# A 1024 x 1024 output projection done with seven block products in place of eight, and a norm's vector kept on chip

## The chip, the cores and the metric

The kernel runs on one core of one Trainium2 chip. A core has TensorE (PE, matrix products into PSUM; PEld is its weight load), VectorE (DVE), ScalarE (ACT), GpSimd (POOL) and SyncE (SP, which here only issues transfers). The metric is the device time of one execution in microseconds (us); lower is better.

## The reference, cut to what matters

One encoder layer is applied to two request groups with the same weights: Prompt (1024 tokens) and Sample (512 tokens), 1024 channels wide, all in float32. The part that the change touches is the end of the layer.

```python
def rms_norm(x, g):
    return x * lax.rsqrt(jnp.mean(x * x, axis=-1, keepdims=True) + EPS) * g
...
    merged = jnp.zeros_like(x)
    for n in range(N_BRANCH):                       # pooling, self-attention, cross-attention
        merged = merged + gates[:, :, n] * (branches[n] @ w_branch[n])    # (L, 512) @ (512, 1024)

    y = rms_norm(merged @ w_out, ln_post)           # (L, 1024) @ (1024, 1024)
    return x + y
```

## The kernel before

Each float32 operand of a product is split into a high part in TensorE's faster format (written by ScalarE, `L168`) and the rest, the low part (written by VectorE as operand minus high part, `L165`). A product then is three matmuls: high x high, high x low, low x high (`mm3`, each 128 x 128 against 128 x 512). `weights` loads a tile of 128 x 1024 weights from memory (`raw<-wt`, `L142`) and splits it into `whi` and `wlo`.

The program is written as one stream of Python generators; a scheduler turns it into a fixed order of instructions for each engine, and every engine works through its own order without overtaking. Priorities (`tc.high_priority`: AHEAD for weight splits, EVAC for emptying PSUM, LATER behind other work) and the number of buffers of each tag (`u`: NU = 7, `med`: NM = 14, `hu`: NHU = 9, `raw`: NRAW = 3, `whi`/`wlo`: NW = 2, `kt`: 4) decide that order. PSUM has three two-bank tiles A and two one-bank tiles B.

The order of the stages is: memory tokens, Prompt's input projections (`products`, which already uses the seven-product form, with additions on the weights in `additions`), Sample's input projections and Prompt's attention woven together, then three blocks of 512 tokens: two of Prompt, one of Sample. A block is `branches` / `merge` (24 steps of 12 matmuls: a step's product, then on VectorE gate times product, `L1080`, then on GpSimd the sum over the branches into `acc`, `L1082`), and `out_phase` (the output projection).

For a Prompt block, `out_phase` takes the output channels in two halves of 512. For each half it goes through four weight tiles (`half`), two k-chunks of 128 channels in each, and four tiles of 128 tokens: 2 x 8 x 4 x 3 = 192 matmuls. `evacuate` multiplies a finished PSUM tile by `lnpost` on VectorE (`L1112`) and squares and sums it on ScalarE (`L1113`). `finish` makes the norm's factor (`L1099`, then GpSimd `L196`, `L200`), multiplies and adds the residual (`L1106`) and stores. The merged operand reaches `out_phase` as eight chunks, split two at a time as they get ready (`split_pair`). `lnpost` is loaded and scaled in each of the three blocks (`L1095`). Sample's block ends in `ending`.

## Time and profile before

| | |
|---|---|
| median of 3 runs | 1457.52 us (1455.51 to 1458.99) |
| the profiled execution | 1455.05 us, of which 1452.8 us are the span that the profile covers |
| mean granted TensorE clock | 0.998 |
| busy share PE / DVE / ACT / POOL | 98% / 67% / 49% / 19% |
| the output projections of Prompt's two blocks | 1183.4 to 1227.0 us and 1292.2 to 1335.8 us of the span |

In the profile an instruction is named by its line, its engine, and output<-input with buffer numbers left out. `med` is a general 128 x 2048 tile: activations, gates, sums and their parts. In the output projection before, `A<-whi,med` is a matmul with a weight part and an activation part. Durations overlap: an instruction's successor on the same engine can start before its recorded end, so the cost of one in a row of many is the distance between starts.

### The profile page before, as it was taken

The numbers are of one execution on the slowest core, as the hardware profiler recorded it, in microseconds if no ns is written. First come the engines' busy times: TensorE is split into PE (matmuls) and PEld (weight loads), VectorE is DVE, ScalarE is ACT, GpSimd is POOL, SyncE is SP. The second block draws the span as 40 slices with busy tenths as digits, with TensorE's granted clock in tenths as the row PEclk, the third lists the DMA queues.
The fourth block names the chain that finished last, engine by engine and source line by source line (L and its number), as shares of the span: only waits on it lengthen the run. The fifth ranks groups of instructions, "written<-read, shape, count | busy, mean of one in ns | idle before, by whom it ended". The sixth has DMA issues, their size and how long they took to land. (4 is left out here: it accounts for less than half of the span.)

```text
span 1452.8 us, 19525 instructions
## 1 busy us (share of the span) xinstructions
PE 1429.2 (98%) x7264; PEld 1198.1 (82%) x7264; DVE 968.9 (67%) x1211; ACT 711.6 (49%) x1085; POOL 276.9 (19%) x286
## 2 busy tenths in 40 slices
PE   7989999999999999999999999999999999999998
PEld 6868888888888888788888888888888888888887
DVE  7996685766547664665777667686676665765764
ACT  6454444444434444443666666676676223323222
POOL 1000110200000000210223332343333230240231
PEclk9999999999999999999999999999999999999999
DMA  8313243332322444244645665565357735945942
GB/s 301 115 60 104 77 138 115 111 123 68 130 97 67 153 140 136 82 157 163 244 187 196 217 231 191 196 224 176 133 170 262 270 121 184 335 161 186 330 139 82
DMA packets 95375, 238.65 MB, mean 164 GB/s; under 512 B 10672, under 2 KB 18992, under 8 KB 95280
## 3 DMA queue, kind: packets, MB, share of 16 engines
q1 hardware_dynamic: 86064, 203.84, 41.5%
q10 hardware_dynamic: 9216, 33.56, 6.0%
q8 instruction: 57, 0.93, 0.3%
q14 instruction: 38, 0.31, 0.1%
HBM read 151.38 MB, written 52.43 MB: 140 GB/s over the span
## 5 line engine op out<-in xcount | busy, mean ns | idle before, releaser
L129 PE MATMUL B<-med,whi 128*128 128x512 f32 x1576 | 493.7, 393 | 5.5 <-DVE med L165 3.0
L129 PE MATMUL A<-med,whi 128*128 128x512 f32 x1200 | 374.1, 392 | 1.6 <-ACT med L168 1.0
L129 PEld LDWEIGHTS B<-med,whi 128*128 128x128 f32 x1576 | 291.9, 188 | 66.0 <-DVE med L165 4.1
L168 ACT ACTIVATE whi<-raw 128x1024 fp32r<-128x1024 f32 (+1 forms) x169 | 167.4, 991 | 289.7 <-PE A L129 137.3
L129 PE MATMUL B<-med,wlo 128*128 128x512 f32 x788 | 308.5, 391 | 0.0
L165 DVE TENSOR_TENSOR wlo<-raw,whi 128x1024 fp32r<-128x1024 f32 (+1 forms) x169 | 211.9, 1255 | 134.7 <-ACT whi L168 133.2
L129 PEld LDWEIGHTS A<-med,whi 128*128 128x128 f32 x1200 | 223.4, 188 | 48.7 <-ACT med L168 1.2
L129 PE MATMUL A<-med,wlo 128*128 128x512 f32 x600 | 234.1, 390 | 0.0
L129 PEld LDWEIGHTS B<-med,wlo 128*128 128x128 f32 x788 | 148.2, 188 | 31.2
L196 POOL TENSOR_SCALAR s<-s 128x16 f32<-128x16 f32 (+3 forms) x17 | 7.5, 442 | 659.1 <-DVE s L591 324.9
L129 PEld LDWEIGHTS A<-med,wlo 128*128 128x128 f32 x600 | 112.8, 188 | 23.9 <-DVE wlo L165 0.2
L165 DVE TENSOR_TENSOR med<-A,med 128x1024 fp32r<-128x1024 f32 (+1 forms) x93 | 112.9, 1215 | 27.7 <-ACT med L168 26.1
L168 ACT ACTIVATE med<-A 128x1024 fp32r<-128x1024 f32 x92 | 94.2, 1025 | 69.2 <-PE A L133 68.8
L823 POOL TENSOR_SCALAR u<-u,s 128x1024 f32<-128x1024 f32 x64 | 72.1, 1126 | 211.9 <-DVE s L822 174.6
L819 DVE TENSOR_REDUCE s<-A 128x1 f32<-128x1024 f32 x64 | 77.8, 1216 | 37.0 <-PE A L129 35.4
L1082 POOL TENSOR_TENSOR med<-med,med 128x512 f32<-128x512 f32 x48 | 75.8, 1592 | 128.0 <-DVE med L1080 90.7
L129 PE MATMUL A<-whi,med 128*128 128x512 f32 (+1 forms) x352 | 98.3, 360 | 0.0
L821 ACT ACTIVATE u<-A,s 128x1024 f32<-128x1024 f32 x64 | 71.4, 1115 | 40.6 <-issue 23.4
L129 PE MATMUL A<-kt,med 128*128 128x512 f32 x320 | 87.8, 395 | 0.0
L168 ACT ACTIVATE whi<-sum 128x1024 fp32r<-128x1024 f32 x50 | 53.1, 1062 | 67.2 <-PE B L129 40.2
L165 DVE TENSOR_TENSOR med<-med,med 128x1024 fp32r<-128x1024 f32 (+1 forms) x50 | 55.1, 1115 | 33.0 <-ACT med L168 29.2
L129 PE MATMUL B<-med,vt 128*128 128x256 f32 x512 | 74.6, 286 | 1.3 <-DVE med L165 1.2
(197 smaller groups left out, 1884.6 us busy)
## 6 DMA issues: line engine op xcount, KB each, us to landing
raw<-wt SPq DMA_DIRECT2D x168, 512.0 KB, 3.7
u<-u ACTq DMA_DIRECT2D x64, 512.0 KB, 3.1
merge<-hu SPq DMA_DIRECT2D x72, 256.0 KB, 2.1
med<-merge SPq DMA_DIRECT2D x72, 256.0 KB, 5.6
med<-br SPq DMA_DIRECT2D x36, 256.0 KB, 5.4
q<-hu SPq DMA_DIRECT2D x24, 256.0 KB, 2.5
br<-hu SPq DMA_DIRECT2D x24, 256.0 KB, 2.9
med<-q SPq DMA_DIRECT2D x12, 512.0 KB, 4.6
```

The source lines that it names most:

```text
L129: pe.matmul(out, l, r, **k)
L165: v.tensor_tensor(out, x, hi.bitcast(F32), op=ALU.subtract)
L168: act.activation(hi, x, AF.Copy)
L196: pool.tensor_scalar(ss, ss, EPS, 1.0, op0=ALU.add, op1=ALU.mult)
L819: v.reduce_max(mx[:], a[:], axis=AX.X, negate=True)
L821: act.activation(p, a[:], AF.Exp, bias=mx[:], accum_out=sm[:])
L823: pool.tensor_scalar(p, p, rc[:], 1.0, op0=ALU.mult, op1=ALU.mult)
L1082: pool.tensor_tensor(at, at, sg, op=ALU.add)
```

## The change

It has two parts. First, for Prompt's two blocks `out_phase` is replaced by `out_products`. Merged (512 tokens x 1024 channels) is taken as four quarters of 256 tokens x 512 channels (a11, a12, a21, a22), the weights as four quarters of 512 x 512, and the result is put together from seven products of quarters. A product is 2 weight tiles x 2 tiles of 128 tokens x 2 k-chunks x 3 = 24 matmuls, 168 in a block. The products need four sums of quarters on the activations (`total`, VectorE, `L1153`), which are then split (`quarter_parts`), and four sums on the weights. The weight sums are computed once, by `out_weights`, as a background task in Prompt's input projections (8 loads, 8 VectorE additions of 128 x 1024, 8 stores to scratch `wsum`), and loaded back in each block by `right`. Partial results are kept in `hu` tiles by ScalarE (`keep`, `L1179`) or added on VectorE (`put`, `L1188`), squared on ScalarE (`L1189`), and multiplied by `lnpost` on GpSimd (`L1190`). The split of the merged operand leaves `merge` except for a11 (`by_quarters`). Second, `lnpost` is loaded and scaled once, into a `sum` tile (`gain`).

```diff
         def gate_to_scratch(m, c0):
             def take(i, j, b, s):
+                if T == 1024 and (m, c0, i, j) == (0, 2, 0, 0):
+                    tasks.append(out_weights())
...
+    wsum = {i: scratch(f"wsum_{i}", [P, 2 * D]) for i in (2, 3, 4, 6)}
+    def out_weights():
+        for c in range(2):
+            b11, b12, b21, b22 = [U() for _ in range(4)]
+            for x, half, k in ((b11, 0, 0), (b12, 1, 0), (b21, 0, 2), (b22, 1, 2)):
+                load(x, wt[TILES["half", half, k + c]])
+            for _ in range(4):
+                yield
+            v.tensor_tensor(b12, b22, b12, op=ALU.subtract)
+            v.tensor_tensor(b11, b12, b11, op=ALU.add)
+            yield
+            v.tensor_tensor(b22, b22, b11, op=ALU.subtract)
+            v.tensor_tensor(b21, b21, b11, op=ALU.subtract)
+            yield
+            for i, x in ((4, b12), (2, b11), (3, b22), (6, b21)):
+                nc.sync.dma_start(wsum[i][:, c * D:(c + 1) * D], x)
...
-        yield from out_phase(merged, xs[g][bs, :], ys[g][bs, :], last)
+        yield from (out_phase if last else out_products)(merged, xs[g][bs, :], ys[g][bs, :])
...
+    def by_quarters(d, acc, merged):
+        if d == 3:
+            merged.append(quarter_parts(quarter(acc, 0, 0)))
+        elif d == 7:
+            merged.append([quarter(acc, i, j) for i in range(2) for j in range(2)])
...
+    def out_products(merged, src, dst):
+        yv, ssq, lnpost = out_tiles()
+        first, (a11, a12, a21, a22) = merged
...
+        def left(i):
+            if i == 1:
+                return quarter_parts(a12)
+            if i == 2:
+                total(3, a21, a22, ALU.add)
+                total(2, sums[3], a11, ALU.subtract)
+            elif i == 4:
+                total(4, a11, a21, ALU.subtract)
+            elif i == 5:
+                total(5, a12, sums[2], ALU.subtract)
+            return quarter_parts(a22 if i == 6 else sums[i])
+        def right(i, c):
+            raw, t = sb.tile([P, D], F32, tag="kt", bufs=4, name=nm("w")), M()
+            load(raw[:], wsum[i][:, c * D:(c + 1) * D] if i in wsum else wt[TILES["half", int(i == 5), c + 2 * (i > 0)]])
+            with tc.high_priority(AHEAD):
+                split(t[:, :D], t[:, D:], raw[:])
...
+        def put(t, n, b, k):
...
+                if k is None:
+                    act.activation(x, b, AF.Copy)
+                else:
+                    v.tensor_tensor(x, b, kept.pop(k)[:], op=ALU.add)
+                act.activation(junk[:], x, AF.Square, scale=0.25 * D ** -0.5, accum_out=ssq[:, t, n:n + 1])
+            pool.tensor_tensor(x, x, lnpost[:, ns], op=ALU.mult)
+        for i in range(7):
+            lhs, bank = ahead, "XYXZXZX"[i]
...
+            for c in range(2):
+                w = right(i, c)
+                if c == 0 and i < 6:
+                    ahead = left(i + 1)
+                for u in range(2):
...
+        for i in range(2):
+            finish(i, yv, ssq, src, dst)
```

How the order of instructions moves is shown at three places of Prompt's first block; the second has the same order.

VectorE, from the gating of the last two merge steps into the output projection. Before (`med_10766` is the low part of merged's last two chunks, `wlo` are weights' low parts):

```order
L1080 SCALAR_TENSOR_TENSOR med_10647<-med_10647,B_10736 128x512
L1080 SCALAR_TENSOR_TENSOR med_10647<-med_10647,A_10751 128x512
L165 TENSOR_TENSOR wlo_10810<-raw_10807,whi_10809 128x1024
L165 TENSOR_TENSOR med_10766<-med_10203,med_10766 128x2x512
L165 TENSOR_TENSOR wlo_10840<-raw_10837,whi_10839 128x1024
L165 TENSOR_TENSOR wlo_10870<-raw_10867,whi_10869 128x1024
L165 TENSOR_TENSOR wlo_10915<-raw_10912,whi_10914 128x1024
L1112 TENSOR_TENSOR med_10769<-A_10775,u_10772 128x512 x2
```

After (`med_10238` and `med_10239` are `acc`; `L1153` are the sums of quarters; `w` is a loaded weight tile; `med_10809` is a12's low part, `med_10825` that of product 0's second weight tile, `med_10848` and `med_10872` those of product 1's two weight tiles):

```order
L1102 SCALAR_TENSOR_TENSOR med_10680<-med_10680,A_10781 128x512
L165 TENSOR_TENSOR wlo_11199<-raw_11196,whi_11198 128x1024
L1153 TENSOR_TENSOR u_10852<-med_10238,med_10239 128x1024
L165 TENSOR_TENSOR med_10809<-med_10239,med_10809 128x1024
L165 TENSOR_TENSOR med_10825<-w_10824,med_10825 128x1024
L165 TENSOR_TENSOR med_10848<-w_10847,med_10848 128x1024
L1153 TENSOR_TENSOR u_10854<-u_10852,med_10238 128x1024
L1153 TENSOR_TENSOR u_10944<-med_10238 128x1024
L1153 TENSOR_TENSOR u_10987<-med_10239,u_10854 128x1024
L165 TENSOR_TENSOR med_10856<-u_10854,med_10856 128x1024
L165 TENSOR_TENSOR med_10872<-w_10871,med_10872 128x1024
```

Nine rows now stand between the gating of the last merge step (with one prefetched split, `wlo_11199`, behind it) and the low part of product 1's second weight tile; the first of them, and all sums, need the complete `acc`.

TensorE at the same place. Before, the last merge matmuls and the first of the projection:

```order
L129 MATMUL A_10751<-med_10603,wlo_10733 128x512
L129 MATMUL A_10751<-med_10603,whi_10732 128x512 x2
L129 MATMUL A_10751<-med_10603,wlo_10733 128x512
L129 MATMUL A_10775<-whi_10779,med_10644 128x512
L129 MATMUL A_10775<-wlo_10780,med_10644 128x512
L129 MATMUL A_10775<-whi_10779,med_10644 128x512 x2
L129 MATMUL A_10775<-wlo_10780,med_10644 128x512
```

After, products 0 and 1 (the name behind the arrow is the weight tile, with both its parts; the second is the activation tile):

```order
L129 MATMUL A_10781<-med_10639,wlo_10763 128x512
L129 MATMUL A_10802<-med_10805,med_10719 128x512 x6
L129 MATMUL A_10803<-med_10805,med_10719 128x512 x6
L129 MATMUL A_10802<-med_10825,med_10719 128x512
L129 MATMUL A_10803<-med_10825,med_10719 128x512
L129 MATMUL B_10845<-med_10848,med_10809 128x512
L129 MATMUL B_10846<-med_10848,med_10809 128x512
L129 MATMUL A_10802<-med_10825,med_10719 128x512 x5
L129 MATMUL A_10803<-med_10825,med_10719 128x512 x5
L129 MATMUL B_10845<-med_10848,med_10809 128x512 x5
L129 MATMUL B_10846<-med_10848,med_10809 128x512 x5
L129 MATMUL B_10845<-med_10872,med_10809 128x512
```

The matmuls of product 0's second weight tile (`med_10825`) and of product 1 follow product 0's first twelve directly; the first of the five (`x5`) is the one that needs a low part.

VectorE at the end of the output projection. Before (`med_11076` and `med_11079` are the low parts of the next block's branch operand):

```order
L1112 TENSOR_TENSOR med_10770<-A_10776,u_10772 128x512
L165 TENSOR_TENSOR med_11076<-med_11068,med_11076 128x2x512
L165 TENSOR_TENSOR med_11079<-med_11068,med_11079 128x2x512
L165 TENSOR_TENSOR wlo_10975<-raw_10972,whi_10974 128x1024
L165 TENSOR_TENSOR wlo_11005<-raw_11002,whi_11004 128x1024
L165 TENSOR_TENSOR wlo_11088<-raw_11085,whi_11087 128x1024
L1112 TENSOR_TENSOR med_10769<-B_10909,u_10772 128x512
L1112 TENSOR_TENSOR med_10769<-B_10910,u_10772 128x512
L1099 TENSOR_REDUCE s_11044<-s_10771 128x2
L1106 SCALAR_TENSOR_TENSOR u_11048<-med_10769,s_11044,u_11048 128x1024
```

After (`med_11148` and `med_11151` are the same low parts, `L1188` adds the two tiles of product 5):

```order
L165 TENSOR_TENSOR med_11050<-w_11049,med_11050 128x1024
L165 TENSOR_TENSOR med_11075<-w_11074,med_11075 128x1024
L165 TENSOR_TENSOR med_11092<-w_11091,med_11092 128x1024
L1188 TENSOR_TENSOR med_10796<-B_10937,hu_10927 128x512
L1188 TENSOR_TENSOR med_10796<-A_10938,hu_10935 128x512
L165 TENSOR_TENSOR med_11148<-med_11140,med_11148 128x2x512
L1226 TENSOR_REDUCE s_11116<-s_10798 128x2
L1233 SCALAR_TENSOR_TENSOR u_11120<-med_10796,s_11116,u_11120 128x1024
L165 TENSOR_TENSOR med_11151<-med_11140,med_11151 128x2x512
```

The low parts of the next block's operand stood ahead of the second half's evacuations; now they stand behind the last addition, and the second one also behind the first multiplication of `finish` (`L1233`), which waits for GpSimd.

More of the change, by code (lines that the diff above doesn't have):

```diff
@@ L1045, in rest @@
                     chunk(order[order.index(n) + 1], d - 2)
-                yield from merge(n, d, gates.pop(i), br, acc, merged if n == order[-1] else None)
+                yield from merge(n, d, gates.pop(i), br, acc, merged, parts if n == order[-1] else None)
         return [partial(chunk, order[0], c) for c in range(4)] + [partial(gate, i) for i in range(2)], rest()
@@ L1092, in out_phase @@
         ssq = S(16)[:].rearrange("p (t q) -> p t q", t=TT)
[L1093 to L1107 removed]
+        if not gain:
+            gain.append(SUM())
+            load(gain[0][:], rows[0:1, 0:D].partition_broadcast(P))
+            v.tensor_scalar_mul(gain[0][:], gain[0][:], 0.25)
@@ new lines, in finish, with out_phase @@
+    def finish(i, yv, ssq, src, dst):
+        ss = S(2)
+        v.reduce_sum(ss[:], ssq[:, 2 * i:2 * i + 2, :2], axis=AX.X)
+        rstd_of(ss[:])
+        with tc.high_priority(-LATER):
+            for j in range(2):
+                t = 2 * i + j
+                x = U()
+                load(x, src[t * P:(t + 1) * P, :])
+                v.scalar_tensor_tensor(x, yv[i][:, j], ss[:, j:j + 1], x, op0=ALU.mult, op1=ALU.add)
+                nc.sync.dma_start(dst[t * P:(t + 1) * P, :], x)
+    def out_phase(merged, src, dst):
+        yv, ssq, lnpost = out_tiles()
@@ L1146, in out_phase @@
-        for i in range(2):
-            finish(i)
+        o = [a[:, i * BLK:(i + 1) * BLK] for a in (A(), A()) for i in range(2)]
+        for c in range(4):
+            w = weights("half", 0, c)
+            for pair in ((0, 1), (2, 3)):
+                for kk in range(2):
+                    k, s = c * 2 + kk, slice(kk * BLK, kk * BLK + BLK)
+                    for t in pair:
+                        ts = slice(t * P, (t + 1) * P)
+                        mm3(o[t][:], (merged[k][0][:, ts], merged[k][1][:, ts]), w(s), k == 0, k == KC - 1)
+                if c == 3:
+                    for t in pair:
+                        evacuate(t, slice(0, BLK), o[t][:], 0)
+                yield
@@ new lines, in out_phase @@
+        av = A()[:].rearrange("p (t n) -> p t n", t=TT)
+        for c in range(2):
+            w = weights("out", 0, c)
+            for kk in range(4):
+                k, s = c * 4 + kk, slice(kk * 256, kk * 256 + 256)
+                for t in range(TT):
+                    ts = slice(t * P, (t + 1) * P)
+                    mm3(av[:, t], (merged[k][0][:, ts], merged[k][1][:, ts]), w(s),
+                        k == 0 and t % 2 == 0, k == KC - 1 and t % 2 == 1)
+                yield
+        for t in range(TT):
+            evacuate(t, slice(512, 768), av[:, t], 1)
@@ L1149, in ending @@
+        yield from ending(merged, src, dst, yv, ssq, lnpost)
     def ending(merged, src, dst, yv, ssq, lnpost):
```

105 lines of the change are left out of this document (54 added, 51 removed).

## The prediction

> **What bounds the kernel now.** I read the page's busy times first, then a table of stretches around Prompt's output projections, then who waited for whom on PE.
>
> ```profile
> span 1452.8 us, 19525 instructions
> PE 1429.2 (98%) x7264; PEld 1198.1 (82%) x7264; DVE 968.9 (67%) x1211; ACT 711.6 (49%) x1085; POOL 276.9 (19%) x286
> ```
>
> ```profile
> core 0: us, PE busy (x) PEld busy (x) DVE busy (x) ACT busy (x) POOL busy (x), PEclk, DMA share, GB/s
> 285.00:345.00 60.00, 60.00 (x278) 49.66 (x277) 35.77 (x50) 26.49 (x39) 4.88 (x5) 1.00 0.31 101
> 1183.40:1227.00 43.60, 43.60 (x194) 36.13 (x193) 20.36 (x21) 15.28 (x24) 4.24 (x4) 1.00 0.46 152
> 1227.00:1292.40 65.40, 65.40 (x290) 54.17 (x289) 47.44 (x48) 20.15 (x22) 23.62 (x17) 1.00 0.76 274
> 1292.40:1336.00 43.60, 43.55 (x192) 35.72 (x191) 20.36 (x21) 16.02 (x24) 4.20 (x5) 1.00 0.46 156
> ```
>
> ```profile
> PE B L129 <- ACT med L168: 0.9, 1, 0.9
> PE B L129 <- DVE med L165: 0.8, 1, 0.8
> ```
>
> In both projections (second and fourth stretch) PE is busy throughout at full clock, DVE for 20.4 of 43.6 us, ACT for 15.3. The last two rows are all that PE waited from 1090 us to the end. So matmuls set the time there, and each one removed is worth a full slot, as long as PE still waits for nothing. A slot comes from the first matmuls of the two projections, one block (192 + 288 = 480 matmuls) apart:
>
> ```profile
> 1183.39 0.39 PE L129 MATMUL A<-whi,med 128*128 128x512 f32 x1
> 1292.19 0.39 PE L129 MATMUL A<-whi,med 128*128 128x512 f32 x1
> ```
>
> 108.80 / 480 = 0.227 us. The recorded 0.39 would overstate it: it ends 0.16 us after the next one starts.
>
> **Matmuls removed.** 24 in each of two blocks: 24 x 0.227 = 5.4 us a block, 10.9 us in all. The projection would need 168 slots, 38.1 us.
>
> **What DVE and ACT must now do in these 38.1 us.** Prices of rows that stand close in a queue are distances between starts:
>
> ```profile
> 1190.36 1.23 DVE L165 TENSOR_TENSOR med<-med,med 128x1024 fp32r<-128x1024 f32 x1 [2.27 <-ACT med L168]
> 1191.50 1.22 DVE L165 TENSOR_TENSOR wlo<-raw,whi 128x1024 fp32r<-128x1024 f32 x1
> 1184.89 0.68 DVE L1080 SCALAR_TENSOR_TENSOR med<-med,B 128x512 f32<-128x512 f32 x1
> 1185.49 0.68 DVE L1080 SCALAR_TENSOR_TENSOR med<-med,A 128x512 f32<-128x512 f32 x1
> 1189.27 1.06 ACT L168 ACTIVATE med<-med 128x1024 fp32r<-128x1024 f32 x1 [4.60 <-POOL med L1082]
> 1190.23 1.05 ACT L168 ACTIVATE whi<-raw 128x1024 fp32r<-128x1024 f32 x1
> 1224.62 0.60 ACT L1113 ACTIVATE hu<-B 128x512 f32<-128x512 f32 x1 [1.89 <-DVE med L1112]
> 1225.22 0.60 ACT L1113 ACTIVATE hu<-B 128x512 f32<-128x512 f32 x1
> ```
>
> A long DVE row (128x1024, a low part or a sum of quarters) costs 1.14 us, a short one from PSUM 0.60, a high part on ACT 0.96, a square with its sum 0.60. From the end of a merge to the end of its projection DVE has 13 weights' low parts, 6 activations' low parts and 4 sums, 23 x 1.14 = 26.2, and 6 additions of 0.60: 29.8 us, against 38.1 for PE. By shares it fits. But these rows stand on PE's path in a fixed order, and the eight multiplications by `lnpost` move to GpSimd, whose rows of this kind collide with DVE's:
>
> ```profile
> 1168.10 1.29 POOL L1082 TENSOR_TENSOR med<-med,med 128x512 f32<-128x512 f32 x1 [1.10 <-DVE med L1080]
> 1168.14 2.33 DVE L165 TENSOR_TENSOR wlo<-raw,whi 128x1024 fp32r<-128x1024 f32 x1 [0.18 <-ACT whi L168]
> 1179.11 3.51 POOL L1082 TENSOR_TENSOR med<-med,med 128x512 f32<-128x512 f32 x2 [3.10 <-DVE med L1080]
> 1179.48 2.00 DVE L165 TENSOR_TENSOR wlo<-raw,whi 128x1024 fp32r<-128x1024 f32 x1
> 1185.71 3.52 POOL L1082 TENSOR_TENSOR med<-med,med 128x512 f32<-128x512 f32 x2 [3.09 <-DVE med L1080]
> ```
>
> A low part that starts 0.04 us behind a GpSimd sum takes 2.33 instead of 1.23; a pair of sums with a low part between takes 3.51 instead of 2.6. They take turns: each costs the other up to 1.29 us. The Trainium skill, "SBUF — State Buffer", section "Who interferes with whom", says that a DVE instruction with two SBUF inputs and a GpSimd one that reads SBUF lock each other out for the whole instruction; by that rule every collision would cost the upper end below. These rows agree; how often they meet, no run here shows yet.
>
> So I follow the printed order, counting from T, the end of the last merge matmul's slot (1183.39 before).
>
> *Stall 1, products 0 and 1.* The last merge result leaves PE 0.16 after T, is gated (0.68, to T+0.9) and added on GpSimd (1.29, to T+2.25). The prefetched low part ahead of the sums collides with that and ends at T+3.4. The nine rows that end with the low part of product 1's second weight take 9 x 1.14 = 10.3, to T+13.6 (ACT's high parts run ahead of them). PE has 36 + 2 slots of work before it needs this part: T+8.6. Stall 5.0 us; 4.0 if the collision is not there. Before, `acc` came later still (the pair of sums of 1185.71 ends at T+5.8), but only the last two of eight chunks waited for it.
>
> *Stall 2, products 2 and 3.* DVE's next row, the addition for product 1, waits for PE: 5 slots and 0.16, T+14.9. Then 0.60 + 1.14 + 0.60 + 1.14 + 1.14 = 4.6 to the low part of product 2's second weight, T+19.5. PE has 10 + 12 + 3 slots from T+13.6: T+19.3. The high part for product 3, which PE wants at T+19.0, comes on ACT at T+19.6 (two squares and three high parts after the first addition), so 0.6 us at least; two GpSimd multiplications fall in here, up to 2.6 more on DVE. Bounds 0.6 to 2.8; taken 1.5, one of the two collisions (19.5 + 1.3 - 19.3), since DVE is busy with such rows about two thirds of that time.
>
> *Stall 3, products 5 and 6.* The same pattern around product 4's additions: DVE needs 4.6 from the first one, PE has 21 slots less the 0.16, 4.6. Bounds 0.3 (ACT's chain: 0.60 + 0.60 + 2 x 0.96 + 0.60 + 0.96 = 4.7 against 4.4) to 2.6 with both collisions; taken 1.3, one of them.
>
> *Stall 4, the next block.* Its second branch low part stands behind the first `finish`, which needs GpSimd's multiplications and these:
>
> ```profile
> L200 POOL TENSOR_TENSOR s<-s,mhalf 128x2 f32<-128x2 f32 x3 | 2.1, 705 | 0.2
> L196 POOL TENSOR_SCALAR s<-s 128x2 f32<-128x2 f32 x3 | 0.6, 191 | 78.8 <-DVE s L1099 78.8
> L1106 DVE SCALAR_TENSOR_TENSOR u<-med,s,u 128x1024 f32<-128x1024 f32 x4 | 5.1, 1282 | 2.2 <-POOL s L200 2.2
> ```
>
> From the end of product 6's last low part: addition 0.60, square 0.60, high part 0.96, square 0.60, multiplication 1.29, factor 0.90, `finish` 1.20, low part 1.14: 7.3 us. PE gets there 5.4 (the lead DVE has without collisions) plus 7 slots, 7.0, later. Bounds 0.5 (the 0.3 and the gaps between rows on three engines) to 2.1 (collisions on this chain, less what they take from the lead); taken 1.3, the middle.
>
> **What is costed at nothing.** `out_weights`: 8 x 1.14 = 9.1 us on DVE, 16 transfers of 512 KB on SP, in the first stretch of the table, where DVE is idle for 24.2 of 60 us and DMA is busy for 0.31. SP issues the weights of the following pair only behind the stored gates:
>
> ```profile
> 306.31 0.33 SPq L142 DMA_DIRECT2D raw<-wt  x1
> 313.80 0.41 SPq L142 DMA_DIRECT2D raw<-wt  x1
> 316.02 0.32 SPq L515 DMA_DIRECT2D merge<-hu  x1
> 331.71 1.23 DVE L165 TENSOR_TENSOR wlo<-raw,whi 128x1024 fp32r<-128x1024 f32 x1 [0.17 <-ACT whi L168]
> ```
>
> The loads of 306.31 and 313.80 move behind the store of 316.02; they land some 5 us later and are first needed at 331.71. Nothing, at most 2 us if an evacuation of PSUM is held up behind an addition that waits for its load. If DVE's gaps were not there, the 9.1 us would show. The single `lnpost`: two loads and two DVE scalings less, beside work that PE does not wait for; 0, at most 1 us gained. The weight transfers of a block rise from 8 to 14 tiles (7.3 MB); they are issued when a `kt` tile is released, 5 to 8 us ahead of need.
>
> ```profile
> DMA to landing us min/median/max: 3.4/5.3/8.4
> ```
>
> This row is for SP's loads from 1183 to 1336 us. At the median they are in time; the slowest would add up to 3 us a block.
>
> **The sum.** A block: -5.44 + 5.0 + 1.5 + 1.3 + 1.3 = +3.66; bounds -5.4 + 5.4 = 0 and -5.4 + 12.5 = +7.1. Two blocks: +7.3 on 1455.05, 1462.4. That execution lies 2.5 below the median of the runs; on the median it is 1464.8. The bounds are 1457.5 and 1471.7, and 2 us more for `out_weights`.
>
> **The rivals.** *VectorE keeps ahead (faster).* DVE's low share in the table speaks for it: if its rows overlapped PE's as before, the whole 10.9 would stay, 1446.6; if only stall 1 stayed, at its 4.0, 1454.6. Against it: the nine rows depend on the complete `acc`, and PE has 8.6 us for what takes 13.6. It decides where all stalls of a block stay under 4.0 us. Chance 0.14.
>
> *Even.* Collisions miss and only the floors remain, 5.4 us a block: 1457.5. Chance 0.20.
>
> *The clock drops in the stalls (slower still).* The clock fell once early in this run, where PE waited in pieces:
>
> ```profile
> 62.00:82.00 20.00, 17.74 (x77) 13.95 (x77) 20.00 (x20) 12.61 (x16) 0.00 (x0) 1.00 0.27 92
> 82.00:90.00 8.00, 6.44 (x24) 4.73 (x23) 7.57 (x9) 4.83 (x6) 0.00 (x0) 0.87 0.21 68
> PE B L129 <- DVE med L165: 2.3, 2, 1.9
> ```
>
> 0.87 over 8 us is 1.0 us lost, and up to 1.7 with what falls beyond; stall 1 comes in similar pieces, but what is lost inside it is covered by DVE's lateness. If it adds 1.7 a block, 1468.2. Chance 0.12. The Trainium skill, "TensorE: Matmul & The Clock Gate", section "HAM oscillation — how this bites in real kernels", asks only that no idle gap exceed about 3.4 us; no single wait above is that long, so by that rule the clock would hold and the sum stay. Here the longest wait near the drop was 1.9 us, so the rule as stated does not cover it.
>
> That the change might not remove the matmuls is excluded by the order.
>
> **The numbers.** The likeliest case, slower by the stalls, has 0.54, with the clock's 0.12 slower 0.66; even 0.20; faster 0.14. About 0.2% (2.9 us) is what a measurement of this kernel can tell from no change. The range runs from 1454 (stall 1 alone at its floor, slightly below) to 1473 (all upper bounds and part of `out_weights`' 2 us); below it lies most of the faster case.
>
> **What would show it.** In the profile after: 48 matmuls fewer; PE waiting in the projections for DVE's and ACT's `med`, some 5 us near the start of each, one to three near products 2 and 5, and about 1 where the next block begins; DVE busy for some 35 us of each projection; DVE low parts of 2 us and more beside GpSimd's L1190; no new PE wait around 285 to 345 us. The prediction is wrong if PE's waits in a projection add up to less than 4 us, or if the time is lost elsewhere, above all to late `w` transfers.

## The result, and the profile after

The changed kernel takes 1474.93 us (median of 4 runs, 1473.12 to 1475.63) where the kernel before takes 1457.64 on the same chip: 1.0118 times as long (95% interval 1.0106 to 1.0130), 17.3 us more. The forecast was 1464.8, range 1454 to 1473. Slower was right; the size was too small by a factor of more than two.

The profiled execution took 1475.63 us, its span is 1473.8. The page's busy times:

```profile
span 1473.8 us, 19557 instructions
PE 1430.1 (97%) x7216; PEld 1191.9 (81%) x7216; DVE 1017.0 (69%) x1239; ACT 736.1 (50%) x1119; POOL 303.4 (21%) x302
```

48 matmuls are gone, as forecast; PE's busy time has not fallen, since slow slots make up for them. Three stretches, of the first projection, the 10 us behind it and the rest of the next block's merge:

```profile
core 0: us, PE busy (x) PEld busy (x) DVE busy (x) ACT busy (x) POOL busy (x), PEclk, DMA share, GB/s
1186.90:1234.00 47.10, 43.79 (x176) 33.09 (x174) 37.73 (x33) 30.58 (x45) 13.05 (x11) 0.96 0.68 231
1234.00:1244.00 10.00, 5.50 (x18) 4.36 (x18) 8.83 (x7) 0.34 (x2) 4.35 (x5) 0.83 0.66 196
1244.00:1303.90 59.90, 59.90 (x266) 49.59 (x265) 40.69 (x39) 17.55 (x18) 22.78 (x15) 1.00 0.70 242
```

Before, PE was busy throughout at full clock (1.00 in these stretches). Now it loses time in the projection and, more densely, in the 10 us behind it: 5.50 of 10 us busy, clock 0.83. What PE waited for from 1090 us to the end (total, times, longest):

```profile
PE B L129 <- DVE med L165: 9.5, 5, 4.5
PE A L129 <- ACT med L168: 3.1, 2, 1.5
PE A L129 <- DVE med L165: 2.2, 4, 0.8
PE B L129 <- ACT med L168: 1.3, 3, 0.9
```

Two single waits of 4.5 us, one in each block, hold over half of it; no wait is for a `w` transfer. PE in order of time, from the projection's first matmul (start, duration, then the idle time ahead):

```profile
1186.85 2.88 PE L129 MATMUL A<-med,med 128*128 128x512 f32 x12
1191.26 0.73 PE L129 MATMUL A<-med,med 128*128 128x512 f32 x2 [1.53 <-ACT med L168]
...
1193.71 4.14 PE L129 MATMUL A<-med,med 128*128 128x512 f32 x10 [0.77 <-DVE med L165]
...
1200.75 2.56 PE L129 MATMUL B<-med,med 128*128 128x512 f32 x10 [0.15 <-DVE med L165]
...
1207.52 2.51 PE L129 MATMUL A<-med,med 128*128 128x512 f32 x10
...
1232.35 0.61 PE L129 MATMUL B<-med,whi 128*128 128x512 f32 x2
...
1238.60 0.79 PE L129 MATMUL B<-med,whi 128*128 128x512 f32 x1 [4.50 <-DVE med L165]
...
1239.62 1.05 PE L129 MATMUL B<-med,whi 128*128 128x512 f32 x2
...
1241.98 0.62 PE L129 MATMUL A<-med,whi 128*128 128x512 f32 x2
```

With slots of 0.227 us these starts give the loss of each part. T is 1186.85.

| part | worked out | loss, us | forecast |
|---|---|---|---|
| 24 matmuls fewer | | -5.4 | -5.4 |
| stall 1 | 38 slots, 8.6, done at T+13.9 | 5.3 | 5.0 |
| stall 2 | 63 slots, 14.3, done at T+20.7, less 5.3 | 1.1 | 1.5 |
| stall 3 | 168 slots, 38.1, done at T+45.5, less 6.4 | 1.0 | 1.3 |
| stall 4, the wait | 1232.35 to 1238.60, less 7 slots | 4.7 | 1.3 |
| slow slots behind it | 1238.60 to 1241.98, less 8 slots | 1.6 | rival, 1.7 |
| a block | | +8.2 | +3.7 |

The two projections begin 117.0 us apart, where it was 108.80: the same 8.2. The second block, up to the first matmul of Sample's projection, takes 118.6 (1303.87 to 1422.47) where it took 109.2 (1292.19 to 1401.37). Together the two are 17.6 us longer in these profiles, which is all of the 17.3.

Of the terms of the sum one is far off, stall 4; behind it stands a loss that the prediction had only as a rival. Its place, DVE and GpSimd at the block's end:

```profile
1223.40 4.58 DVE L165 TENSOR_TENSOR med<-w,med 128x1024 fp32r<-128x1024 f32 x3
...
1230.99 1.97 POOL L1190 TENSOR_TENSOR med<-med,sum 128x512 f32<-128x512 f32 x1 [0.27 <-ACT hu L1189]
...
1234.00 3.46 POOL L1190 TENSOR_TENSOR med<-med,sum 128x512 f32<-128x512 f32 x2
1234.06 2.28 DVE L1233 SCALAR_TENSOR_TENSOR u<-med,s,u 128x1024 f32<-128x1024 f32 x1 [2.19 <-POOL s L200]
1236.26 2.28 DVE L165 TENSOR_TENSOR med<-med,med 128x1024 fp32r<-128x1024 f32 x1
```

The second branch low part (1236.26) is the one that PE waits for. It stands behind `finish` (1234.06), which stood idle 2.19 us for GpSimd's factor, and both then run beside product 6's two multiplications (1234.00) and take 2.28 us each, where rows alone take 1.23 to 1.28.

### The profile page after: what moved, and what is told of

Same layout as the page of the kernel before. It is cut to its first block, busy times and chain, and to the rows that moved or that the text cites. A ratio compares the mean times of both kernels' runs of the same rounds, so it can differ in the third digit from the quotient of the medians.

```text
span 1473.8 us, 19557 instructions
## 1 busy us (share of the span) xinstructions
PE 1430.1 (97%) x7216; PEld 1191.9 (81%) x7216; DVE 1017.0 (69%) x1239; ACT 736.1 (50%) x1119; POOL 303.4 (21%) x302
## 4 chain that ended last, share of the span: by engine, by line
PE 42%; DVE 3%; DMA 2%; ACT 2%; issue 1%; POOL 1%; SPq 0%; DVEq 0%; ACTq 0%; POOLq 0%
PE B L129 23%; PE A L129 15%; PE A L133 4%; DVE med L165 1%; ACT med L168 1%; DMA u<-mv 0%; DMA w<-wsum 0%; DMA u<-u 0%; ACT hu L1189 0%; DVE wlo L165 0%; DMA hu<-x_gate 0%; POOL med L1190 0%; DVE med L1188 0%; DMA hu<-xq 0%; ACT whi L168 0%
## 5 line engine op out<-in xcount | busy, mean ns | idle before, releaser
L168 ACT ACTIVATE whi<-raw 128x1024 fp32r<-128x1024 f32 (+1 forms) x153 | 150.5, 984 | 288.7 <-PE A L129 155.2
L165 DVE TENSOR_TENSOR wlo<-raw,whi 128x1024 fp32r<-128x1024 f32 (+1 forms) x153 | 196.4, 1285 | 102.6 <-ACT whi L168 100.9
L168 ACT ACTIVATE med<-A 128x1024 fp32r<-128x1024 f32 x92 | 94.1, 1024 | 68.8 <-PE A L133 68.3
L1104 POOL TENSOR_TENSOR med<-med,med 128x512 f32<-128x512 f32 x48 | 72.8, 1526 | 132.8 <-DVE med L1102 132.8
L165 DVE TENSOR_TENSOR wlo<-sum,whi 128x1024 fp32r<-128x1024 f32 x50 | 61.1, 1222 | 23.0 <-ACT whi L168 22.1
L129 PEld LDWEIGHTS B<-med,vt 128*128 128x128 f32 x512 | 65.7, 188 | 3.9 <-DVE med L165 1.4
```

What stands on the lines that cost most here:

```text
L129: pe.matmul(out, l, r, **k)
L165: v.tensor_tensor(out, x, hi.bitcast(F32), op=ALU.subtract)
L168: act.activation(hi, x, AF.Copy)
L1104: pool.tensor_tensor(at, at, sg, op=ALU.add)
```

## The experiments

In the table, "a block" is the distance between the first matmuls of the two projections in the profile, so it is the first block alone; the second can differ (118.6 after 117.0 in the changed kernel). Ratios are to the kernel before, run on the same chip. e2 and e4 leave out work whose result is needed; the others leave out nothing.

| kernel | median, us | ratio (95% interval) | a block, us |
|---|---|---|---|
| before | 1456.4 to 1457.6 | | 108.8 |
| changed | 1474.9 | 1.0118 (1.0106 to 1.0130) | 117.0 |
| e1 sums and vector alone | 1455.9 | 0.9995 (0.9986 to 1.0003) | 108.8 |
| e2 no GpSimd multiplication | 1461.9 | 1.003 (1.002 to 1.004) | 110.9 |
| e3 finish later | 1465.3 | 1.0049 (1.0034 to 1.0065) | 112.2 |
| e4 no weight low parts | 1455.4 | 0.9989 (0.9981 to 0.9998) | 107.9 |
| e5 weights first | 1472.2 | 1.0092 (1.0072 to 1.0112) | 116.6 |
| e7 loads late | 1475.7 | 1.0118 (1.0098 to 1.0137) | 118.1 |
| e8 factor in finish | 1461.1 | 1.0029 (1.002 to 1.0037) | 110.4 |
| e10 fifth second | 1473.1 | 1.0104 (1.0091 to 1.0117) | 115.3 |
| e11 and its banks | 1459.8 | 1.0019 (1.001 to 1.0028) | 109.6 |
| e12 e8 and loads late | 1460.2 | 1.002 (1.0011 to 1.0028) | 110.7 |
| e14 e8, weights behind gate | 1457.1 | 1.0002 (0.9991 to 1.0012) | 107.7 |
| e15 e14, additions later | 1456.6 | 0.9994 (0.9982 to 1.0005) | 111.3 (its slowest execution, 1460.3) |
| e16 e14, first addition later | 1456.5 | 0.9998 (0.9989 to 1.0006) | 108.6 |
| e17 e11, weights ahead | 1455.3 | 0.9989 (0.998 to 0.9997) | 106.6 |
| e19 e17, banks paired anew | 1457.6 | 1.0009 (1.0 to 1.0018) | 108.6 |

### The end of a block

**e2**, GpSimd's multiplication taken out:

```diff
-            pool.tensor_tensor(x, x, lnpost[:, ns], op=ALU.mult)
```

> The changed kernel (1474.9 us) without GpSimd's eight multiplications by the norm's vector in each of the two projections; that factor is left out of Prompt's output. Nothing else moves in the order of DVE, ACT or PE. Theory A (the fixed order of DVE's rows behind the finished sum and behind the first finish sets the stalls): only stall 4 shortens, since the first finish still waits for the squares and GpSimd's factor but no longer for multiplications queued ahead of the factor (some 2 us) nor for the 1 us that its low part loses beside them; 1474.9 - 2 x 3 = 1469. Theory B (the collisions of GpSimd's multiplications with DVE's low parts set them): low parts of 1.6 to 2.3 us in the projection fall to 1.2, stalls 2, 3 and 4 all shrink, 2 x 5 less or more: at most 1465. If neither holds, 1474.

**e3**, the multiplication kept, `finish` put behind the next block's second branch low part:

```diff
-        for i in range(2):
-            finish(i, yv, ssq, src, dst)
+        pending.extend(partial(finish, i, yv, ssq, src, dst) for i in range(2))
...
                     br = split_pair(t[:, :D]) + split_pair(t[:, D:])
+                    with tc.issue_after(lows[0].ins):     # the last low part
+                        while pending:
+                            pending.pop(0)()
```

> The changed kernel with both finish steps of a block tied behind the second low part of the next block's first branch, so that this low part stands directly behind the first one on DVE; the multiplications on GpSimd stay. Theory A (order of the rows): the second low part comes at about 1231.8 + up to 2.3 in the profile's time where it ended at 1238.5, PE's wait of 4.5 us at each block's end falls below 0.5, and the slices with a clock of 0.78 behind it go: 4.3 + 1.7 a block, 1474.9 - 12 = 1463; without the clock's part 1466. Theory B (collisions): the low part collides with the GpSimd multiplications wherever it stands, PE still waits 2 us or more: 1470 or above.

Measured: 1461.9 and 1465.3. By the numbers, e2 missed theory A's 1469 and came out as theory B had it (at most 1465), and e3 came out as theory A had it. In both, PE loses only some 0.3 us at the branch low part. DVE there, first e2, then e3:

```profile
1231.73 1.29 DVE L1232 SCALAR_TENSOR_TENSOR u<-med,s,u 128x1024 f32<-128x1024 f32 x1 [1.11 <-POOL s L200]
1232.94 1.22 DVE L165 TENSOR_TENSOR med<-med,med 128x1024 fp32r<-128x1024 f32 x1
```

```profile
1232.41 3.70 DVE L167 TENSOR_TENSOR med<-med,med 128x1024 fp32r<-128x1024 f32 x2 [1.15 <-ACT med L170]
```

So it takes both causes: the place behind `finish` *and* GpSimd's rows. In e2 the low part still stands behind `finish`, but ends at 1234.2, just when PE gets there (1234.1); `finish` and the low part take 1.29 and 1.22 there, where beside GpSimd they took 2.28 each. e2 also takes the multiplications themselves out of the chain, so it does not separate their own time from the collisions; the row times do. In e3 it still collides (two rows 3.70 instead of 2.35), but no longer waits for the factor. Either edit alone takes the whole stall and the slow slots, 6.1 and 4.8 us a block. Of PE's other waits e2 leaves 1.5, 0.8 and 0.3 as they were, and its projection still takes 45.3 us for 45.5: theory B holds for stall 4, but that collisions set stalls 2 and 3 too falls. What e3 gives back is a wait of 1.0 for a `wlo`, since two `finish` rows beside GpSimd now take 4.54 us.

**e8** does both without leaving anything out: the factor and the vector in one DVE row of `finish`, the residual in a second, and these rows stand one by one behind the gating rows of the next block.

```diff
-                v.scalar_tensor_tensor(x, yv[i][:, j], ss[:, j:j + 1], x, op0=ALU.mult, op1=ALU.add)
+                v.scalar_tensor_tensor(yv[i][:, j], yv[i][:, j], ss[i][:, j:j + 1], lnpost, op0=ALU.mult, op1=ALU.mult)
+                v.tensor_tensor(x, yv[i][:, j], x, op=ALU.add)
```

> The changed kernel with GpSimd's multiplications gone from the projection: each finish step multiplies y by the factor and the norm's vector in one DVE instruction and adds the residual in a second, 8 DVE rows of 1.14 to 1.2 us a block in place of 4, tied one by one behind the gating steps of the next block. From the two single edits (without the multiplications 1461.9, finish later 1465.2): stall 4 goes, no collision is left in the projection, stalls 1 to 3 stay at 110.9 - 103.4 = 7.5 a block; 1461. Rival: the 9 us of DVE rows make the next block's weights late (the finish later alone shows a wait of 1.0 for one): up to 2 us a block more, 1465.

1461.1, as expected. From here on stall 4 is out of the way.

### The beginning of the projection

**e4**, the weights' low parts left out on DVE:

```diff
-                split(t[:, :D], t[:, D:], raw[:])
+                act.activation(t[:, :D], raw[:], AF.Copy)
```

> The changed kernel without the low parts of the projection's weights (the high part is used in their place, so the matmuls and their number stay; the low parts are left out of the result). DVE loses 14 rows of 1.14 us in each projection, ACT nothing. Theory A (DVE's row order and lateness): stalls 1 to 3 (some 8 us a block with the slow clock) nearly go; stall 4 stays at 4.5 and its slow slices at 1.7, since its chain has no weight in it: 1474.9 - 2 x 7 = 1461. Rival: ACT's high parts and the loads are as late, then at most 2 us a block go: 1471 or above.

1455.4: more than expected, since the wait of 4.5 went as well. PE's longest wait for DVE in the blocks is 0.8:

```profile
PE B L129 <- DVE med L165: 2.8, 4, 0.8
```

Stall 4's chain starts with DVE's addition for product 5, which stands behind low parts of weights (1223.40 above): with these gone it starts earlier. So DVE's rows lie behind stall 4 as well. What is left, a block of 107.9 against 103.4 for 456 slots, lies in two places: 2.5 us in the projection, with the wait of 1.5 for a high part behind the complete sum, and 2.1 at the block's end, where each of the branch's two low parts now stands behind a `finish`:

```profile
1229.56 0.50 PE L129 MATMUL B<-med,whi 128*128 128x512 f32 x1 [0.77 <-DVE med L165]
...
1231.89 0.51 PE L129 MATMUL B<-med,whi 128*128 128x512 f32 x1 [0.68 <-DVE med L165]
```

**e5** issues the four weight tiles of products 0 and 1 at the projection's start:

```diff
+        ws = {ic: right(*ic) for ic in ((0, 0), (0, 1), (1, 0), (1, 1))}
...
-                w = right(i, c)
+                w = ws[i, c] if i < 2 else right(i, c)
```

> The changed kernel with the loads and splits of the first two products' four weight tiles issued at the start of the projection, so that ACT's and DVE's rows for them stand ahead of the merge's last rows instead of behind the finished sum. Theory A: products 0 and 1 no longer wait for a weight (0.2, 0.8 and the 0.15 of stall 1 go, and with them the slow slots between); left are the low part of the second quarter, due at T+5.4 and done at about T+5.7, and the weight of product 2 behind product 1's additions, at T+12.8 against 10.9: 2 to 3 us where stalls 1 and 2 now take about 8; 1474.9 - 2 x 5 = 1465. Theory B (collisions): the four low parts now meet GpSimd's sums of the merge instead and lose up to 1.1 us each, which delays the finished sum as much: 1471 or above.

1472.2: a miss of theory A, B was right. GpSimd's sums and PE's first wait in e5:

```profile
1185.02 4.38 POOL L1104 TENSOR_TENSOR med<-med,med 128x512 f32<-128x512 f32 x2 [1.82 <-DVE med L1102]
1191.22 2.11 POOL L1104 TENSOR_TENSOR med<-med,med 128x512 f32<-128x512 f32 x1 [1.82 <-DVE med L1102]
1194.48 0.73 PE L129 MATMUL B<-med,med 128*128 128x512 f32 x2 [2.36 <-ACT med L168]
```

The low parts stood ahead of the merge's last gating rows and met its sums. The last gating row starts at T+3.9 (1190.41) instead of T+0.2, the last sum takes 2.11 instead of 1.29, and `acc` is complete at T+6.8, not T+2.3. So it was queueing as well as collisions. The stall moved from the weight to the activations.

**e14**, on e8: the same weights, but tied *behind* the last gating row.

```diff
+        ws = {(0, 0): right(0, 0)}
+        with tc.issue_after(anchor[0].ins):               # the last gating row on DVE
+            ws.update({ic: right(*ic) for ic in ((0, 1), (1, 0), (1, 1))})
```

> The kernel of the factor in the finish (1461.1, a block 110.4), with the splits of products 0 and 1's weights standing directly behind the merge's last gating row: ahead of the rows that need the complete sum (unlike in the changed kernel), yet behind the gating (unlike when only moved to the front, which put the sum off). Theory A: of stall 1's 5.3 us 4 go, but the additions for product 1 now wait ahead of product 2's low parts, some 2 us come back: a block 108 to 109, 1457. Rival (collisions with the merge's last GpSimd sums eat it, as before): 1460 or above.

```profile
1194.11 5.32 PE L129 MATMUL B<-med,med 128*128 128x512 f32 x22 [0.64 <-DVE med L165]
...
1202.11 5.29 PE L129 MATMUL A<-med,med 128*128 128x512 f32 x22 [1.83 <-DVE med L165]
```

1457.1, as expected: 0.64 is left of stall 1, and 1.83 came back at product 2. The same rows in another order: the order of DVE's rows around T is enough to make stall 1 or to take most of it, without a change in their number.

### Work beside the path

**e1** adds `out_weights` and the single vector to the kernel before:

```diff
+                if T == 1024 and (m, c0, i, j) == (0, 2, 0, 0):
+                    tasks.append(out_weights())
...
-        lnpost = U()
+        if not gain:
+            gain.append(SUM())
```

> The kernel before, with only the side work of the change: the weight sums (8 additions on DVE, 16 transfers of 512 KB) made at the same place as in the change but never read, and the last norm's vector loaded once. The old projection stays. The prediction costed both at nothing (0 to 2 us, and 0 to -1): 1457 to 1458. Rival (theory D): they are what makes the first projection begin 3.5 us later in the profile of the changed kernel, then 1460 to 1461.

1455.9, ratio 0.9995 with an interval that holds 1: they cost nothing that can be told here. **e7** (and **e12**, the same on e8) has the first w loads late:

```diff
-            load(raw[:], wsum[i][:, c * D:(c + 1) * D] if i in wsum else wt[...])
+            with tc.issue_after(marks[0].ins) if i < 2 else nullcontext():
+                load(raw[:], wsum[i][:, c * D:(c + 1) * D] if i in wsum else wt[...])
```

> The changed kernel with the four first w loads of the first block (512 KB each) tied behind the load of the first gate of the second branch, so that they are issued after about 1100 us instead of between 940 and 1000. Theory D (these early transfers crowd the loads of the cross-attention): the waits of PE at 968.6 and 1032.9 go and block 1 begins 2.3 us earlier: 1472.6. Rival: those waits come from elsewhere and nothing moves, 1474.9, or the loads now come too late and a wait of 1 us or more for a w tile appears at the block's start: 1476.

> The kernel of the factor in the finish (1461.1), with the four first w loads of the first block tied behind the load of the second branch's first gate. Theory D: the loads between 940 and 1000 us cost the cross-attention 2.2 us (the profile of the late loads alone had the first projection 576.7 us behind the wait at 608-610 us, the changed kernel 579.0, the kernel before 575.1): 1459. Rival: these differences lie between executions of one kernel: 1461.

e7: 1475.7, no gain. e12: 1460.2 against e8's 1461.1; their intervals to before overlap. So no effect shows in the total time. Theory D rested on one profile of each kernel, so both were profiled again.

> The kernel before, unchanged, profiled again. If the first projection again begins 575 us behind the wait near 608 us, the change delays it by 2 to 4 us (theory D in some form); if it begins 576 to 579 us behind it, this lies between executions and is no part of the change's 17.3 us.

> The same once more: a second draw of that distance, 575 if the change is what delays it, up to 579 if executions differ.

> The changed kernel, unchanged, profiled again: the distance again, 579.0 if it is the change's, 576 to 579 if executions differ; and whether the waits of a block repeat: 1.5, 0.2 and 0.8 in stall 1, 4.5 at the end, 117.0 us between the projections' beginnings.

The wait near 608 us and the projection's first matmul, in the two new profiles of before:

```profile
607.27 0.73 PE L129 MATMUL B<-med,whi 128*128 128x512 f32 x2 [1.31 <-ACT med L449]
1188.52 0.39 PE L129 MATMUL A<-whi,med 128*128 128x512 f32 x1
```

```profile
608.54 0.73 PE L129 MATMUL B<-med,whi 128*128 128x512 f32 x2 [1.33 <-ACT med L449]
1184.49 0.39 PE L129 MATMUL A<-whi,med 128*128 128x512 f32 x1
```

581.3 and 576.0, after 575.1 in the first profile; the changed kernel 579.0 and 577.7. This distance differs by 6.2 us between executions of one unchanged program, so it cannot decide theory D. The wait of PE near 968 us can. SP issues w loads at 959.55 in the changed kernel, and 0.3 us later ACT issues a transfer of the self-attention, `u<-u`. In e12 these loads come later. The transfer, the time that two of its kind take to land, and PE's matmuls that need it, first in the changed kernel, then in e12:

```profile
959.86 0.49 ACTq L852 DMA_DIRECT2D u<-u  x1
DMA to landing us min/median/max: 3.5/6.1/8.6
968.61 0.86 PE L133 MATMUL A<-identr,u 128*128 128x128 f32 x8 [1.09 <-DVE s L1009]
```

```profile
959.76 0.47 ACTq L852 DMA_DIRECT2D u<-u  x1
DMA to landing us min/median/max: 4.0/4.2/4.5
967.25 0.80 PE L133 MATMUL A<-identr,u 128*128 128x128 f32 x8
```

The transfer lands after 8.6 us and after 4.5: at 968.5, just ahead of PE's start, and at 964.3. All twenty profiles divide the same way. In the fourteen with the early loads it takes 8.0 to 8.9 us and PE waits there, 0.5 to 1.4 us; in the six without (three of before, e1, e7, e12) it takes 4.1 to 4.6 and PE does not wait. (The profile names the transfer as what ended the wait in ten of the fourteen. In the other four it names a DVE row that ended at about the same time, but in e12 PE starts before that row.) So theory D holds for this wait, though the transfer belongs to the self-attention: the early loads cost about 1 us ahead of the first projection, and e7 and e12 take that away. It is too little to show in the medians. The second wait that e7 named (1032.9) is no part of it: it stands in a profile of before as well (1.3 us).

A block repeats better than that distance: 108.8 in all three profiles of before, 117.0 and 118.4 in the changed kernel, whose two blocks together are 17.6 and 17.4 us longer than the 218.0 of before.

### Another order of the products

**e10**, on e8: product 4's operand (`a11 - a21`) is complete four merge steps early, so it comes second.

```diff
+            v.tensor_tensor(x, quarter(acc, 0, 0), quarter(acc, 1, 0), op=ALU.subtract)    # at d == 3
+            merged.append(quarter_parts(x))
...
-            lhs, bank = ahead, "XYXZXZX"[i]
+        turn = (0, 4, 1, 2, 3, 5, 6)
+            lhs, bank = ahead, "XYXZWZW"[i]
```

> The kernel of the factor in the finish, with the products in another order: the fifth product (first quarter less third, times a weight sum), whose quarters are complete four merge steps earlier, comes second, in a PSUM pair of its own, and the four weight tiles of the first two products are split ahead of the block's last rows. Everything that needs the complete sum has 24 slots, 5.4 us, more. It costs two ACT copies and four short DVE additions a block. Theory A: stall 1 (5.3 us) goes, and DVE's lead carries into stall 2; a block takes 103.4 + 0.5 to 2 = 104 to 105.5 where before takes 108.8: 1457 - 2 x 4 = 1449. Rival (collisions): the early splits meet GpSimd's sums and delay the complete sum, as they did when only moved (wait of 2.4): but it is needed 5.4 us later, so this alone cannot take it back; if other rows are late in its place, 1455 or above.

1473.1, a miss, for a reason of the edit itself: both token tiles of X were halves of one PSUM tile, so PE's matmuls into the second half waited for ACT's copy of the first, and that copy stood on ACT behind a row that waited for `acc`. `acc` was late, too: complete at 1196.44, T+8.4 with this run's T of 1188.03 (the T+9.6 in e11's expectation counts from the changed kernel's T).

```profile
1199.01 6.86 PE L129 MATMUL A<-med,med 128*128 128x512 f32 x20 [5.84 <-ACT hu L1188]
```

**e11** pairs X with Y in a tile, takes two single banks for W, and puts product 4's weights behind the gate.

```diff
+        both = [A() for _ in range(2)]
+        banks = {"X": [a[:, :BLK] for a in both], "W": [B()[:] for _ in range(2)], "Y": [a[:, BLK:] for a in both]}
```

> The kernel with the fifth product second, mended in two places that its trace showed: the two halves of a PSUM pair are taken from different tiles, so that PE no longer waits for the copy of one half (5.8 us in each block) before it writes the other, and the splits of the fifth product's weights stand behind the merge's last gating row, so that the complete sum is no longer put off to T+9.6. If PSUM's sharing and the late sum were all that was wrong, a block takes 104 to 106 us where before takes 108.8: 1457 - 2 x 4 = 1449, at most 1453. Rival: other rows are late, a block stays above 108: 1457 or more.

1459.8. The order on ACT is next: a weight's high part stood behind one that waits for a sum (1200.42) and behind a copy.

```profile
1200.42 1.06 ACT L168 ACTIVATE med<-u 128x1024 fp32r<-128x1024 f32 x1 [3.91 <-DVE u L1162]
...
1202.96 0.49 PE L129 MATMUL A<-med,med 128*128 128x512 f32 x1 [2.35 <-ACT med L168]
```

**e17** issues that weight ahead as well:

```diff
         with tc.issue_after(anchor[0].ins):
-            ws.update({ic: right(*ic) for ic in ((4, 0), (4, 1))})
+            ws.update({ic: right(*ic) for ic in ((4, 0), (4, 1), (1, 0), (1, 1))})
```

> The kernel with the fifth product second and its banks mended (a block 109.6, 1459.8), with product 1's two weight tiles split on ACT and DVE directly behind the fifth product's, instead of behind the row that waits for the complete sum. Theory A (order): the waits of 2.3 and 0.8 us in each block go; 109.6 - 3.4 = 106.2, 1459.8 - 7 = 1453. Theory E (the loads, since no w tile can be loaded before another has been split): the wait moves to a DMA or to a later weight, a block stays above 108.5: 1458 or above.

```profile
1205.49 0.47 PE L129 MATMUL A<-med,med 128*128 128x512 f32 x1 [1.16 <-DVE med L1197]
1206.54 11.26 PE L129 MATMUL A<-med,med 128*128 128x512 f32 x48 [0.57 <-DVE med L165]
```

1455.3, the best of all: 0.9989 (0.998 to 0.9997), 1.6 us below before, which is less than the 0.2% that the prediction took as the limit. The block came out as theory A said (106.6 for 106.2), but the time did not (1455.3 for 1453). Its two blocks take 213.3 us for 218.0, 4.7 less, in a profile that is only 0.5 us shorter (1454.6 for 1455.1): its first projection begins 4.3 us later, at 1187.72 for 1183.39. The wait near 968 us is 1.4 of that (this kernel has the early loads); before's own profiles begin it between 1183.4 and 1188.5, so what the rest is stays open. **e19** pairs X with W instead, and puts product 1's addition behind product 2's low parts as in e16 below:

```diff
-        banks = {"X": [a[:, :BLK] for a in both], "W": [B()[:] for _ in range(2)], "Y": [a[:, BLK:] for a in both]}
+        banks = {"X": [a[:, :BLK] for a in both], "W": [a[:, BLK:] for a in both]}
```

> The fastest version so far (1455.3, a block 106.6) with the PSUM banks paired so that product 2 no longer shares a tile with product 1, whose addition now stands behind product 2's low parts. The waits of 1.2 us for that addition and of 0.6 for the low part behind it should go in each block: a block 104.8 to 105.5, 1455.3 - 2 x 1.5 = 1452, some 0.3% less than before. Theory E (the loads are next): the block stays above 106.2, 1455.

1457.6, a miss: product 4's first matmul now shares a tile with the copy of product 0, and ACT reaches that copy late, behind two splits that waited for their loads.

```profile
1190.53 1.06 ACT L170 ACTIVATE med<-w 128x1024 fp32r<-128x1024 f32 x1 [1.84 <-DMA w<-wt]
1193.21 1.06 ACT L170 ACTIVATE med<-w 128x1024 fp32r<-128x1024 f32 x1 [1.62 <-DMA w<-wt]
...
1195.92 7.34 PE L129 MATMUL A<-med,med 128*128 128x512 f32 x24 [2.73 <-ACT hu L1191]
```

**e15** and **e16**, on e14, put PSUM-emptying additions behind the next product's low parts (all that can wait, or product 1's alone):

```diff
-                            put(u, 0, b[u], (0, u))
+                            later.append(partial(put, u, 0, b[u], (0, u)))
...
+                if c == 1 and later:
+                    with tc.issue_after(lows[0].ins):
+                        while later:
+                            later.pop(0)()
```

> The same, and the additions that empty products 1, 4 and 5 (which nothing waits for in the next 24 slots) stand behind the next product's low parts instead of ahead of them, and the sums for products 4 and 5 behind the weights of products 3 and 4. Theory A says that all of DVE's lateness behind T comes from rows that stand ahead of the rows PE needs, so nearly all waits in the projection go: a block 103.4 + 0.5 to 2, 1457 - 2 x 4 = 1449. If the shares of DVE or the transfers set the time instead of the order, a block stays above 107: 1455 or above.

> The kernel with the weights behind the gate (block 107.7, 1457.1), and of the later additions only those for product 1 (and the two sums for products 4 and 5): they stand behind product 2's low parts. The additions for products 4 and 5 stay where they were. Theory A (order): of the 1.8 us for which PE waited ahead of product 2 in each block 1.1 go, as in the kernel with all additions later, and the slow slots behind it; nothing is given back at the block's end; a block 105.5 to 106.5, 1457.1 - 2 x 1.7 = 1454. Theory E (the loads): the w tiles that are released earlier are loaded earlier and put off the next block's branch, which ACT then waits for; a block stays at 107.7 or more: 1457 or above.

1456.6 and 1456.5: the waits they aimed at fell (1.83 to 0.71), but the time did not. In e15's profile, its slowest execution (1460.3; they reach down to 1452.8), ACT waits at the block's end for the next block's branch:

```profile
1229.24 1.06 ACT L170 ACTIVATE med<-med 128x1024 fp32r<-128x1024 f32 x1 [2.57 <-DMA med<-br]
```

In e16 the waits that are gone at product 2 are partly back as 0.5 and 0.3 later on. Whether loads are the next bound stays open: e15 and e19 show waits for them, no run took a load away.

## Why the prediction was wrong, step by step

- *Slower, because DVE's rows stand on PE's path in a fixed order:* right. e4 (fewer rows) and e14 (other order, on e8) each come back to the time of before.
- *Slots:* -5.4 a block, right; 48 matmuls fewer.
- *Stalls 1, 2, 3:* 5.3, 1.1, 1.0 for 5.0, 1.5, 1.3. The low part of product 1's second weight ended at T+13.9 for a forecast T+13.6. That stall 1 comes in pieces with slow slots whose loss DVE's lateness covers was right in the first block: PE begins the second weight of product 1 at T+13.9, and in e3, where the same slots ran at full speed, at T+13.7. In the second block it was not: the slots were slower still, and PE got there at T+14.8.
- *Stall 4:* **the step that failed**, 4.7 for 1.3, outside its bounds of 0.5 to 2.1. The chain was named right, but it was mis-sized: each row was priced as if alone, 7.3 us, with PE due after 7.0, and the upper bound left 1.6 for collisions. It took 10.6 (1227.91, the start of the row behind the last of the three low parts, to 1238.54): the multiplication 1.97 for 1.29, `finish` 2.28 for 1.20, the low part 2.28 for 1.14, and 0.4 in gaps. PE was due after 6.0 instead of 7.0, since the three low parts ahead had collided too (4.58). 10.6 - 6.0 is 4.6. It was no accident of one execution: the same wait is 4.50 and 4.55 in the two blocks of this profile, 4.58 and 4.54 in the second one. The prediction counted the multiplications that the chain waits for, but not product 6's two, which stand on GpSimd right behind the factor: the factor's end starts them and `finish` at the same moment (1234.00 and 1234.06). The Trainium skill, "SBUF — State Buffer", section "Who interferes with whom", which the prediction drew on, says that such rows lock each other out; the 2.28 and 2.28 agree.
- *The clock:* a rival with a chance of 0.12 that came true. The prediction looked for the drop in stall 1's pieces; it came there, too (0.58, last section), but the loss stands behind stall 4. That its price fits in the first block (1.6 for 1.7) is luck: the 1.7 was read from another stage, and in the second block the same loss is 2.4. The Trainium skill, "TensorE: Matmul & The Clock Gate", section "HAM oscillation — how this bites in real kernels", gives a gap of about 3.4 us, and the drop behind 4.5 us here agrees. The section behind it in the Trainium skill, "A second HAM failure mode: psum-queue depth-cycling", tells of short idles between groups of matmuls; that fits the drop behind 1.53 and 0.77 us, but not that the same waits left the clock alone in e3 (last section).
- *`out_weights`, the single vector, the transfers at nothing:* right for the first two (e1). No wait of PE for a `w` shows in the profile after, but the first `w` loads of the block cost about 1 us elsewhere: they are issued more than 200 us ahead of need and delay a transfer of the self-attention (e7, e12).
- *The range:* its upper bounds added 12.5 us of losses to a block; 13.7 came. What lay outside is stall 4 with its slow slots. The prediction's sign "PE's waits in a projection add up to less than 4 us" also came: the profile's waits there are 3.2 us. The other 4.3 of the 7.4 us lost in the first projection are slow slots, which the sum had not set apart from waits.

## What to carry to other kernels

Where a row that the bottleneck engine waits for stands behind a chain over two other engines, list everything that the chain's events release on those engines at the same moment: what starts together collided each time here (a wait of 4.5 us in all four blocks of two profiles), not with some chance. And count, for an engine with a low busy share, the rows between the event that completes an operand and the row that is waited for: here a DVE that was busy for 69% of the span cost 8.2 us in the first block, and moving rows (and the multiplication by the norm's vector to DVE) took it back. Moving a row ahead helps only as long as it does not push back what completes the operand (e5), and each gain exposes the next row in line.

## What the runs showed of the hardware

The clock can drop without one long wait, and not each time. In the changed kernel's stall 1 the ten matmuls behind the third wait took 4.14 us (1193.71 above), and the granted clock there was 0.58. In e3 they stand behind the same waits (1.52, 0.22, 0.77) and took 2.57 us, at a clock of 1.00. The stretches, first the changed kernel's, then e3's with its row:

```profile
1193.60:1197.70 4.10, 3.99 (x11) 3.12 (x12) 4.10 (x5) 1.54 (x2) 0.00 (x0) 0.58 0.59 183
```

```profile
1196.02 2.57 PE L129 MATMUL A<-med,med 128*128 128x512 f32 x10 [0.77 <-DVE med L167]
1196.00:1200.00 4.00, 3.98 (x17) 3.30 (x18) 4.00 (x4) 2.33 (x4) 0.00 (x0) 1.00 0.62 182
```

Over both blocks of the seven profiles with such waits (changed twice, e2, e3, e7, e8, e12) the ten slots ran at full speed in two of fourteen cases, 2.4 us from first start to the next matmul, and took 3.4 to 4.4 in the others. What tells them apart no run here shows. Behind the single wait of 4.50 us the granted clock in the changed kernel fell to 0.57 over the next 4 us:

```profile
1238.00:1242.00 4.00, 3.40 (x9) 2.69 (x10) 2.90 (x4) 0.00 (x0) 0.89 (x2) 0.57 0.94 307
```

A transfer took twice as long to land, 8.0 to 8.9 us for 4.1 to 4.6, when two loads of 512 KB each were issued at about the same time on another queue (e7 above). And the stretch from the wait near 608 us to the first projection differed by 6.2 us between three executions of one unchanged program (575.1, 576.0, 581.3), so a shift of that size between two single profiles says nothing.
